# Gate and up products of the first 512 tokens between the attention steps of the last two token groups

## The chip, the cores and the metric

The kernel runs on one core of a Trainium2 chip. The metric is the device time of one execution in microseconds; before the change it is 2694.07 us, the median of three runs (2692.1 to 2694.11). PE is TensorE (PEld its weight loads), DVE is VectorE, ACT is ScalarE, POOL is GpSimd, and SP issues all the DMAs.

## What is computed

One layer of a hybrid encoder on 2048 tokens of width 1024, in float32: a normed input goes through one projection to a gated linear recurrence and to a stick-breaking attention with 8 heads of 64; both results are normed, projected and added to the input; then comes a gated feed-forward part with 2816 hidden channels and a last norm. Cut to what matters here:

```
h  = rms_norm(x) ;  u = h @ W_in                          # 1024 -> 2560
y  = concat(rms_norm(gelu(gate) * rg_lru(...)), rms_norm(stick_breaking_attention(q, k, v)))
x2 = x + y @ W_out
h2 = rms_norm(x2) ;  gu = h2 @ W_ffn_in                   # 1024 -> 2 * 2816
x3 = x2 + (silu(gu[:, :2816]) * gu[:, 2816:]) @ W_ffn_out
out = rms_norm(x3)
```

## The kernel before

Every float32 operand of a product is split into a high and a low part, and `mm3` (L115 to L118) takes three products for one: high by high, high by low, low by high.

The tokens are worked on in 4 groups of 512 (`GT`), g = 0 to 3. `prep(g)` takes the projections and the recurrence of a group. `attention(g)` takes its attention: an item is 128 queries of a head against up to 512 keys, and there are 32, 64, 96 and 128 items in the groups 0 to 3. For an item `score` (L317) makes the tile z on PE, ACT makes u and be of it by two sigmoids, `scan` (L336) runs the product of u along the keys on DVE, `weights` (L342) multiplies be by it on DVE, `turn` (L347) transposes be in 128x128 blocks on PE into t, which ACT (ah) and DVE (al) split, and `weigh` (L365) multiplies by the values on PE into y. `LAGS` says how many items score and scan run ahead of turn.

`drive` (L429) writes the steps of attention(g) and spreads units of other work, the fill, evenly between them. A unit is what the fill's generator does up to a `yield`. On PE the order stands as it is written; on the other engines a scheduler sets it. The fill of attention(0) to attention(2) is prep(1) to prep(3). The fill of attention(3) is `mix_out` (L668): for every group and branch but the last one it takes x + norm(y) @ W_out in `Mix.run` (L624), 32 units of 6 matmuls with 256 columns (tile po), and after a group's second branch `store_rows` (L655) writes the rows to DRAM (`x2_d`) and takes their norms (`rsf`). `next_half` (L225) hands out half a group of weight columns and starts the load of the half that is used two later (`AHEAD`); a half is 128x1024, loaded (raw), copied by ACT (hi) and subtracted by POOL in four pieces (lo), or loaded in its parts where an earlier use has kept them in DRAM.

After the attention the last branch is mixed, and the feed-forward part runs over two halves of 1024 tokens (`half`, each two groups of 512). `make_h2` (L752) loads, scales, transposes (h2t) and splits the rows of a half. For each of the 22 column tiles f, `gate_up` (L817) takes gate (j = 0) and up (j = 1): a 128x1024 tile of weights (gur, split into guh and gul by `split_gu`, L779) by both groups of the half, 24 matmuls with 512 columns into pgu for each group. Then silu, the product and its split into ahi and alo follow. `down` (L848) takes the second product (pw) for two column tiles at a time, one such pair behind `gate_up`. The weight tiles have three buffers (`wgu`), the raw tile has one.

```
        for g in range(NG - 1):
            drive(attention(g), prep(g + 1), n_prep - (g + 2 == NG) * LESS)
        n_out = 2 * TPG * (D // WC)
        drive(attention(NG - 1), mix_out(*first), n_out * (2 * NG - 1) + WAIT)
```

## Time and profile before

| | us |
|---|---|
| median of the timed runs | 2694.07 |
| span of the profiled execution | 7685.8 |
| PE busy in the profile | 7656.3 (100%) |
| DVE, ACT, POOL busy in the profile | 1421.4, 1124.6, 896.9 |

The profiled execution is 2.85 times as long as the timed ones. Its stretches, by the first scan of each group, are: start and prep(0) to about 460 us, attention(0) to 943, attention(1) to 1655, attention(2) to 2499, attention(3) to 3679, the last branch to 3789, the feed-forward part to the end. The durations that the profile gives for DVE, ACT and POOL are those of single instructions; how the ones of PE are to be read is a question of its own, since PE fills the whole span.

### The profile page before, as it was taken

How to read it: one execution, taken by the hardware profiler on the slowest of the kernel's cores; microseconds unless marked ns; L12 is line 12 of the kernel's file. 1: busy time of each engine (PE TensorE's matmuls, PEld its weight loads, DVE VectorE, ACT ScalarE, POOL GpSimd, SP SyncE). 2: the span in 40 equal slices, each digit the busy share in tenths (PEclk: the TensorE clock that was granted, in tenths of full speed). 3: DMA queues.
4: the chain of work that ended last, by engine and by line, in shares of the span. 5: the costliest groups of instructions: out<-in, count | busy, mean ns of one | idle time of the engine just before them, and what ended most of it. 6: DMA issues, size and time to landing. Idle time of an engine off the chain costs nothing.

```text
span 7685.8 us, 36652 instructions
## 1 busy us (share of the span) xinstructions
PE 7656.3 (100%) x13472; PEld 5024.0 (65%) x13472; DVE 1421.4 (18%) x2278; ACT 1124.6 (15%) x2024; POOL 896.9 (12%) x1261
## 2 busy tenths in 40 slices
PE   9999999999999999999999999999999999999999
PEld 5665676767676888888755555555555555555555
DVE  1112222223333333333100000000011000000002
ACT  2112212222222222222100000000011000000001
POOL 2211101100001110000010111111111111111111
DMA  3222222121111222211200000000011000000000
GB/s 106 78 82 73 92 71 69 59 71 55 56 59 61 68 76 66 76 50 49 79 19 14 19 19 18 18 19 19 17 36 55 19 19 17 19 19 19 17 17 25
DMA packets 167445, 350.05 MB, mean 46 GB/s; under 512 B 17504, under 2 KB 58464, under 8 KB 167264
## 3 DMA queue, kind: packets, MB, share of 16 engines
q1 hardware_dynamic: 167264, 347.70, 13.7%
q8 instruction: 106, 1.74, 0.1%
q14 instruction: 75, 0.61, 0.0%
HBM read 268.20 MB, written 79.43 MB: 45 GB/s over the span
## 4 chain that ended last, share of the span: by engine, by line
PE 100%; DVE 0%; DMA 0%; SPq 0%; issue 0%; ACT 0%
PE pgu L116 11%; PE pgu L117 11%; PE pgu L118 11%; PE y L375 6%; PE z L325 6%; PE t L360 6%; PE pw L117 6%; PE pw L116 5%; PE pj L116 5%; PE pj L118 5%; PE pw L118 5%; PE pj L117 5%; PE po L116 3%; PE po L117 3%; PE po L118 3%; PE pv L117 1%
## 5 line engine op out<-in xcount | busy, mean ns | idle before, releaser
L116 PE MATMUL pgu<-hhi,guh 128*128 128x512 f32 x1408 | 1201.0, 853 | 0.0
L117 PE MATMUL pgu<-hlo,guh 128*128 128x512 f32 x1408 | 1200.2, 852 | 0.0
L118 PE MATMUL pgu<-hhi,gul 128*128 128x512 f32 x1408 | 1200.1, 852 | 0.0
L116 PEld LDWEIGHTS pgu<-hhi,guh 128*128 128x128 f32 x1408 | 505.8, 359 | 363.1 <-issue 361.6
L117 PEld LDWEIGHTS pgu<-hlo,guh 128*128 128x128 f32 x1408 | 505.2, 359 | 360.6 <-issue 360.6
L118 PEld LDWEIGHTS pgu<-hhi,gul 128*128 128x128 f32 x1408 | 503.7, 358 | 362.9 <-issue 358.7
L116 PE MATMUL pj<-ht_hi,w_hi 128*128 128x512 f32 x512 | 601.0, 1174 | 0.0
L117 PE MATMUL pw<-dnl,ahi 128*128 128x512 f32 x704 | 587.9, 835 | 0.0
L118 PE MATMUL pw<-dnh,alo 128*128 128x512 f32 x704 | 587.6, 835 | 0.0
L116 PE MATMUL pw<-dnh,ahi 128*128 128x512 f32 x704 | 586.5, 833 | 0.0
L118 PE MATMUL pj<-ht_hi,w_lo 128*128 128x512 f32 x512 | 559.7, 1093 | 0.0
L117 PE MATMUL pj<-ht_lo,w_hi 128*128 128x512 f32 x512 | 559.0, 1092 | 0.0
L325 PE MATMUL z<-ks,qd 128*128 128x512 f32 (+2 forms) x640 | 552.6, 998 | 0.0
L360 PE MATMUL t<-ident,be 128*128 128x128 f32 x1088 | 534.3, 690 | 0.0
L830 DVE TENSOR_TENSOR sg<-pgu,sg 128x512 f32<-128x512 f32 x88 | 60.9, 692 | 2530.6 <-PE pgu L118 2516.7
L860 DVE TENSOR_TENSOR x<-pw,x 128x512 f32<-128x512 f32 x352 | 243.4, 692 | 987.0 <-PE pw L118 987.0
L360 PEld LDWEIGHTS t<-ident,be 128*128 128x128 f32 x1088 | 270.8, 249 | 234.2 <-issue 160.4
L785 POOL TENSOR_TENSOR gul<-gur,guh 128x1024 fp32r<-128x1024 f32 x88 | 208.0, 2364 | 1729.8 <-ACT guh L784 1635.4
L375 PE MATMUL y<-al,vs 128*128 128x256 f32 x576 | 395.7, 687 | 0.0
L375 PE MATMUL y<-ah,vs 128*128 128x256 f32 x576 | 395.0, 686 | 0.0
L116 PE MATMUL po<-wo_hi,yhi 128*128 128x256 f32 x512 | 384.2, 750 | 0.0
L118 PEld LDWEIGHTS pw<-dnh,alo 128*128 128x128 f32 x704 | 249.6, 355 | 172.8 <-issue 172.4
(183 smaller groups left out, 7820.4 us busy)
## 6 DMA issues: line engine op xcount, KB each, us to landing
gur<-in_w_gu SPq DMA_DIRECT2D x88, 512.0 KB, 3.4
w_hi<-w_d SPq DMA_DIRECT2D x50, 512.0 KB, 3.3
w_lo<-w_d SPq DMA_DIRECT2D x50, 512.0 KB, 4.6
dnr<-in_w_dn SPq DMA_DIRECT2D x88, 256.0 KB, 2.6
vs<-vs_d SPq DMA_DIRECT2D x80, 256.0 KB, 3.0
ks<-ks_d SPq DMA_DIRECT2D x80, 256.0 KB, 3.0
qd<-q_d SPq DMA_DIRECT2D x128, 128.0 KB, 2.8
w_raw<-in_w_in SPq DMA_DIRECT2D x30, 512.0 KB, 4.3
```

Source lines behind the costliest of these rows:

```text
L116: nc.tensor.matmul(ps, lhsT=w_hi, rhs=m_hi, start=first, stop=False)
L117: nc.tensor.matmul(ps, lhsT=w_hi, rhs=m_lo, start=False, stop=False)
L118: nc.tensor.matmul(ps, lhsT=w_lo, rhs=m_hi, start=False, stop=last)
L325: nc.tensor.matmul(z[:, :nz], lhsT=qd[:, i, qs], rhs=kss[p.c][:, :nz], start=i == 0, stop=i == 1)
L360: nc.tensor.transpose(tp[:, b, :], p.be[s][:, b * P:(b + 1) * P], ident)
L375: nc.tensor.matmul(y, lhsT=vs[:, b, :], rhs=t[:, b].rearrange("p s q -> p (s q)"), start=first and m == 0, stop=last and m == 1)
L785: nc.gpsimd.tensor_tensor(out=wlo, in0=raw, in1=f32(whi), op=ALU.subtract)
L830: nc.vector.tensor_tensor(out=sg, in0=pss[1, g], in1=sg, op=ALU.mult)
L860: nc.vector.tensor_tensor(out=x2[t][:, ns], in0=ps, in1=x2[t][:, ns], op=ALU.add)
```

## The change

The gate and up products of group 0, 22 x 2 x 24 matmuls with 512 columns, leave the feed-forward part. `gate_up_first` is a new piece of the fill: after the second branch of group 0 it scales the rows that are still on chip, transposes and splits them through `make_ht` (with the other gain and the tiles of the mixer), and takes the products of all 22 column tiles with weights from `next_half`; the gate is x * sigmoid(x) with ACT's sigmoid and one more product on DVE. The results go to `act_d` in DRAM, 256 KB each. The feed-forward part leaves group 0 out of `make_h2` and of the products and loads the results from `act_d`. The weights of the first half of the tokens are therefore loaded and split once more than before.

`mix_out` with `gate_up_first` now starts in attention(2): `OVER` = 96 units of it follow prep(3) there (4 empty ones, 64 of the branches of group 0, 8 of transposes and 20 of gate and up), and the rest, 332 units of gate and up and 160 of the other branches, is spread over attention(3), which had 228 units before. A unit of gate and up is 3 matmuls with 512 columns.

```diff
+OVER = 96
+    act_d = [dram.tile([P, GT], F32, name=f"act_d{f}") for f in range(NF)]
...
-    def make_ht(g, xs):
+    def make_ht(g, xs, gain=None):
+        gain = gm if gain is None else gain
...
-        nc.sync.dma_start(out=raw, in_=src)
+        dst = raw if src.shape[1] == KD // 2 else \
+            raw.rearrange("p k c -> p (k c)").rearrange("p (k c) -> p k c", c=src.shape[2])
+        nc.sync.dma_start(out=dst, in_=src)
...
+        if g == 0:
+            queue += [(w_gu[f, j], f"wgu{f}_{j}", ("gu", f, j), False) for f in range(NF) for j in range(2)]
...
-    def drive(steps, fill, n_fill):
+    def drive(steps, fill, n_fill, rest=True):
...
-        for _ in fill:
+        for _ in fill if rest else ():
             pass
...
+                    if self.rs is None:
+                        self.sums()
                     nc.vector.scalar_tensor_tensor(out=x2[t][:, ns], in0=po, scalar=self.rs[:, t:t + 1],
...
+    def gate_up_first(x2, last):
+        for t in range(TPG):
+            r = rsf[:, t:t + 1]
+            if t % 2:
+                nc.scalar.activation(x2[t], x2[t], AF.Copy, scale=r)
+            else:
+                nc.vector.tensor_scalar(out=x2[t], in0=x2[t], scalar1=r, scalar2=None, op0=ALU.mult)
+        yield from make_ht(NG, x2, gf)
+        for f in range(NF):
+            pss = []
+            for j in range(2):
+                hi, lo = (t.rearrange("p k c -> p (k c)").rearrange("p (k c) -> p k c", c=P) for t in next_half())
+                ps = ps_d.tile([P, GT], F32, tag="d", name=f"pgf{f}_{j}")
+                pss.append(ps)
+                for k in range(KD):
+                    mm3(ps, hi[:, k], lo[:, k], *hts[NG][k], k == 0, k == KD - 1)
+                    if k < KD - 1:
+                        yield
+                    elif (f, j) == (NF - 1, 1):
+                        last()
+                if j == 0:
+                    sg = stg.tile([P, GT], F32, tag="s", name=f"sgf{f}")
+                    nc.scalar.activation(sg, ps, AF.Sigmoid)
+                    nc.vector.tensor_tensor(out=sg, in0=ps, in1=sg, op=ALU.mult)
+                else:
+                    nc.vector.tensor_tensor(out=sg, in0=ps, in1=sg, op=ALU.mult)
+                    nc.sync.dma_start(out=act_d[f], in_=sg)
+                yield
...
-            yield from cur.run(x2, following, NCT if i + 2 < len(jobs) else NCT - 1)
+            gated = (g, br) == (0, 1)
+            yield from cur.run(x2, None if gated else following, NCT if i + 2 < len(jobs) else NCT - 1)
             if br == 1:
                 store_rows(g, x2)
+            if gated:
+                yield from gate_up_first(x2, lambda: [following.take(c) for c in range(NCT)])
...
-        for g in range(NG - 1):
-            drive(attention(g), prep(g + 1), n_prep - (g + 2 == NG) * LESS)
+        for g in range(NG - 2):
+            drive(attention(g), prep(g + 1), n_prep)
+        def filling():
+            yield from prep(NG - 1)
+            yield from mix_out(*first)
+        fill = filling()
+        drive(attention(NG - 2), fill, n_prep - LESS + OVER, rest=False)
...
-        drive(attention(NG - 1), mix_out(*first), n_out * (2 * NG - 1) + WAIT)
+        drive(attention(NG - 1), fill, n_out * (2 * NG - 1) + WAIT + KD + 2 * NF * KD - OVER)
...
+                if g == 0:
+                    hs.append(None)
+                    continue
...
-                for g, (hi, lo) in enumerate(hs):
+                for g, h in enumerate(hs):
+                    if h is None:
+                        continue
...
-                nc.scalar.activation(sg, pss[0, g], AF.Silu)
-                nc.vector.tensor_tensor(out=sg, in0=pss[1, g], in1=sg, op=ALU.mult)
+                if hs[g] is None:
+                    nc.sync.dma_start(out=sg, in_=act_d[f])
+                else:
+                    nc.scalar.activation(sg, pss[0, g], AF.Silu)
+                    nc.vector.tensor_tensor(out=sg, in0=pss[1, g], in1=sg, op=ALU.mult)
```

PE in the middle of attention(3), head 2, from one item's transposes to the next one's. Before, with branch 1 of group 0 as the fill:

```order
L360 MATMUL t3_2_0_2_0_11317<-ident_60,be3_2_0_2_0_11170 128x128 x4
L116 MATMUL po0_1_1_2_11290<-wo0_1_3_hi_10748,yhi0_1_0_1_10161 128x256
L117 MATMUL po0_1_1_2_11290<-wo0_1_3_lo_10749,yhi0_1_0_1_10161 128x256
L118 MATMUL po0_1_1_2_11290<-wo0_1_3_hi_10748,ylo0_1_0_1_10162 128x256
L116 MATMUL po0_1_1_2_11290<-wo0_1_3_hi_10748,yhi0_1_1_1_10168 128x256
L117 MATMUL po0_1_1_2_11290<-wo0_1_3_lo_10749,yhi0_1_1_1_10168 128x256
L118 MATMUL po0_1_1_2_11290<-wo0_1_3_hi_10748,ylo0_1_1_1_10169 128x256
L325 MATMUL z3_2_0_0_0_11333<-ks3_2_0_10559,qd3_2_10542 128x512 x2
L360 MATMUL t3_2_0_2_1_11340<-ident_60,be3_2_0_2_1_11201 128x128 x4
```

The same place on PE after the change, with the up product of column tile 9 (pgf9_1) as the fill:

```order
L368 MATMUL t3_2_0_2_0_12172<-ident_60,be3_2_0_2_0_12017 128x128 x4
L119 MATMUL pgf9_1_12188<-ht_hi4_0_10327,wgu9_1_hi_11987 128x512
L120 MATMUL pgf9_1_12188<-ht_lo4_0_10328,wgu9_1_hi_11987 128x512
L121 MATMUL pgf9_1_12188<-ht_hi4_0_10327,wgu9_1_lo_11988 128x512
L119 MATMUL pgf9_1_12188<-ht_hi4_1_10348,wgu9_1_hi_11987 128x512
L120 MATMUL pgf9_1_12188<-ht_lo4_1_10349,wgu9_1_hi_11987 128x512
L121 MATMUL pgf9_1_12188<-ht_hi4_1_10348,wgu9_1_lo_11988 128x512
L119 MATMUL pgf9_1_12188<-ht_hi4_2_10365,wgu9_1_hi_11987 128x512
L120 MATMUL pgf9_1_12188<-ht_lo4_2_10366,wgu9_1_hi_11987 128x512
L121 MATMUL pgf9_1_12188<-ht_hi4_2_10365,wgu9_1_lo_11988 128x512
L333 MATMUL z3_2_0_0_0_12201<-ks3_2_0_11417,qd3_2_11400 128x512 x2
L368 MATMUL t3_2_0_2_1_12208<-ident_60,be3_2_0_2_1_12043 128x128 x4
```

Between the two transposes stood 6 fill matmuls with 256 columns, and now there are 9 with 512.

PE at the place in attention(2) where the fill goes over from the second branch of group 0 (po0_1) to the transposes of its scaled rows (htp4, xo0), after the change:

```order
L119 MATMUL po0_1_1_3_10217<-wo0_1_3_hi_9764,yhi0_1_3_1_9308 128x256
L120 MATMUL po0_1_1_3_10217<-wo0_1_3_lo_9765,yhi0_1_3_1_9308 128x256
L121 MATMUL po0_1_1_3_10217<-wo0_1_3_hi_9764,ylo0_1_3_1_9309 128x256
L178 MATMUL htp4_0_10329<-ident_60,xo0_0_9135 128x128
L178 MATMUL htp4_0_10329<-ident_60,xo0_1_9137 128x128
L178 MATMUL htp4_0_10329<-ident_60,xo0_2_9139 128x128
L178 MATMUL htp4_0_10329<-ident_60,xo0_3_9141 128x128
L333 MATMUL z2_7_1_2_0_10337<-ks2_7_2_9552,qd2_7_9547 128x384 x2
```

The transposes stand directly behind the product whose result they turn, with no attention step between the two.

## Rows read from the trace of the kernel before

**Rows 1.** The page's head and PE's own busy time in it
```profile
span 7685.8 us, 36652 instructions
...
PE 7656.3 (100%) x13472; PEld 5024.0 (65%) x13472; DVE 1421.4 (18%) x2278; ACT 1124.6 (15%) x2024; POOL 896.9 (12%) x1261
```
**Rows 2.** Timeline in attention(3): start us, length us, engine, line, tiles, count
```profile
3001.27 3.10 PE L618 MATMUL pss<-ones,acc 128*128 128x1 f32 x8
```
**Rows 3.** Costliest PE groups: forms, count | busy us, mean ns | idle before
```profile
L116 PE MATMUL pgu<-hhi,guh 128*128 128x512 f32 x1408 | 1201.0, 853 | 0.0
...
L116 PE MATMUL pj<-ht_hi,w_hi 128*128 128x512 f32 x512 | 601.0, 1174 | 0.0
L117 PE MATMUL pw<-dnl,ahi 128*128 128x512 f32 x704 | 587.9, 835 | 0.0
...
L360 PE MATMUL t<-ident,be 128*128 128x128 f32 x1088 | 534.3, 690 | 0.0
...
L325 PE MATMUL z<-ks,qd 128*128 128x512 f32 x448 | 433.0, 1101 | 0.0
L375 PE MATMUL y<-al,vs 128*128 128x256 f32 x576 | 395.7, 687 | 0.0
...
L116 PE MATMUL po<-wo_hi,yhi 128*128 128x256 f32 x512 | 384.2, 750 | 0.0
```
**Rows 4.** Busy time by stretch: attention(2), attention(3), feed-forward part
```profile
core 0: us, PE busy (x) PEld busy (x) DVE busy (x) ACT busy (x) POOL busy (x), PEclk, DMA share, GB/s
...
1655.00:2499.00 844.00, 844.00 (x1503) 573.43 (x1502) 272.15 (x370) 203.59 (x382) 82.78 (x224) 1.00 0.18 58
2499.00:3679.00 1180.00, 1180.00 (x2644) 1017.33 (x2643) 402.11 (x634) 262.85 (x517) 95.26 (x263) 1.00 0.19 65
...
3789.00:7686.00 3897.00, 3886.89 (x6400) 2274.84 (x6399) 351.79 (x604) 294.71 (x453) 462.86 (x292) 1.00 0.07 23
```
**Rows 5.** PE groups by form in attention(3), 2499 to 3679 us
```profile
L116 PE MATMUL po<-wo_hi,yhi 128*128 128x256 f32 x448 | 337.9, 754 | 0.0
...
L360 PE MATMUL t<-ident,be 128*128 128x128 f32 x474 | 229.3, 685 | 0.0
L325 PE MATMUL z<-ks,qd 128*128 128x512 f32 x208 | 199.9, 1097 | 0.0
L375 PE MATMUL y<-ah,vs 128*128 128x256 f32 x252 | 173.0, 687 | 0.0
```
**Rows 6.** PE groups by form in attention(2), 1655 to 2499 us
```profile
L360 PE MATMUL t<-ident,be 128*128 128x128 f32 x337 | 165.6, 694 | 0.0
L116 PE MATMUL pj<-ht_hi,w_hi 128*128 128x512 f32 x126 | 155.5, 1234 | 0.0
...
L375 PE MATMUL y<-ah,vs 128*128 128x256 f32 x176 | 120.8, 686 | 0.0
```
**Rows 7.** Groups on POOL, ACT and DVE that the change adds or repeats
```profile
L785 POOL TENSOR_TENSOR gul<-gur,guh 128x1024 fp32r<-128x1024 f32 x88 | 208.0, 2364 | 1729.8 <-ACT guh L784 1635.4 <-DMA x_d<-xo 94.4
...
L196 POOL TENSOR_TENSOR w_lo<-w_raw,w_hi 128x256 fp32r<-128x256 f32 x120 | 90.5, 784 | 245.6 <-ACT w_hi L193 245.6
...
L830 DVE TENSOR_TENSOR sg<-pgu,sg 128x512 f32<-128x512 f32 x88 | 60.9, 692 | 2530.6 <-PE pgu L118 2516.7 <-ACT guh L784 13.9
...
L193 ACT CAST w_hi<-w_raw 128x1024 fp32r<-128x1024 f32 x30 | 31.1, 1045 | 84.8 <-PE pj L117 66.9 <-PE pv L118 9.2 <-issue 8.4
```
**Rows 8.** Timeline at the start of the feed-forward part, DVE and SP
```profile
3788.86 0.75 DVE L638 SCALAR_TENSOR_TENSOR xo<-po,ry_y,xo 128x512 f32<-128x512 f32 x1 [9.02 <-PE po L118]
...
3793.04 0.17 DVE L665 COPY rsf<-rf_y 128x4 f32<-128x4 f32 x1
...
3794.63 4.20 SPq L872 DMA_DIRECT2D x<-x_d  x8
...
3799.86 0.33 SPq L781 DMA_DIRECT2D gur<-in_w_gu  x1
```

**Rows 9.** DMA issues on the page: count, KB each, median us to landing
```profile
gur<-in_w_gu SPq DMA_DIRECT2D x88, 512.0 KB, 3.4
```

More of the change, by code (lines that the diff above doesn't have):

```diff
@@ L174, in make_ht @@
                 nc.tensor.transpose(tp[:, t * P:(t + 1) * P], xs[t][:, k * P:(k + 1) * P], ident)
-            nc.scalar.activation(hi, tp, AF.Copy, scale=gm[:, k:k + 1])
-            nc.vector.scalar_tensor_tensor(out=lo, in0=tp, scalar=gm[:, k:k + 1], in1=f32(hi),
+            nc.scalar.activation(hi, tp, AF.Copy, scale=gain[:, k:k + 1])
+            nc.vector.scalar_tensor_tensor(out=lo, in0=tp, scalar=gain[:, k:k + 1], in1=f32(hi),
                                            op0=ALU.mult, op1=ALU.subtract)
@@ L622, in sums @@
             self.rs = rsqrt_mean(ss, TPG, LRU, f"ry{self.nm}")
+        rs = None
         def run(self, x2, following=None, ready=NCT):
@@ L757, in make_h2 @@
             yield hs
-            for gl, (hi, lo) in enumerate(hs):
+            for gl, h in enumerate(hs):
+                if h is None:
+                    continue
+                hi, lo = h
                 g = half * (HT // GT) + gl
@@ L820, in gate_up @@
                 whi, wlo = early.pop((half, f, j), None) or load_gu(half, f, j)
-                for g, (hi, lo) in enumerate(hs):
+                for g, h in enumerate(hs):
+                    if h is None:
+                        continue
+                    hi, lo = h
                     ps = pss[j, g] = ps_g.tile([P, GT], F32, tag="p", name=f"pgu{half}_{f}_{j}_{g}")
```

## The prediction

> **What bounds the kernel now.** I read the page's head first, and it does not fit the times: the span is 7685.8 us, PE is busy in all of it [rows 1], and the timed runs take 2694.07 us. So the next question is what a PE duration in this profile means. A timeline in attention(3) tells: eight matmuls with a single column take 3.10 us, 0.39 us each [rows 2]. 13472 matmuls [rows 1] at 0.39 us would be 5254 us, twice the timed runs. The profiled execution thus has a cost per PE instruction that the timed ones cannot have. PE's busy share, and every wait for PE, is a product of the profiling here and tells nothing of the timed runs. The reader who takes "PE 100%" at its word would say that moving PE work gains nothing; that is a rival below.
>
> What holds in both are instruction counts, shapes, and the lengths on DVE, ACT and POOL. So I price PE by columns. The large groups have 2.16 (pgu, three lines of 1408), 1.08 (pw), 0.79 (pj), 0.14 (t), 0.23 (z), 0.29 (y, two lines of 576) and 0.39 million columns (po) [rows 3]; pv and other small groups add 0.34 by the code's loops: 5.42 million. **Upper price:** PE cannot work for longer than the run, so a column costs on average at most 2694.07 us / 5.42 million = 0.497 ns. **Lower price:** the stretches show a granted clock of 1.00 [rows 4], the 2.4 GHz level; one column in one of its cycles would be 0.417 ns. No row shows that it is one cycle, so I keep both ends. At the lower price PE works 2259 us and is idle for 435 us; at the upper one never.
>
> Where could it be idle? attention(3): po has 1344 matmuls of 256, t 474 of 128, z 208 of 512 (and some shorter), y 504 of 256 [rows 5], in all 0.66 million columns, 276 to 330 us. DVE is busy there for 402.11 us [rows 4]. attention(2): pj 378 of 512, t 337, y 352 [rows 6], with z, pv and small ones by the code 0.48 million columns, 199 to 238 us, against 272.15 us on DVE [rows 4]. In the feed-forward part it is the other way: 3.24 million columns, 1352 to 1612 us, against 351.79 us on DVE [rows 4]. So in the last two groups of attention DVE needs longer than PE at either price, and in the feed-forward part PE is alone. The floors of the two groups are DVE's 402 + 272 = 674 us, of which PE stands for 106 (upper price) to 199 us (lower).
>
> **The change part by part.** *Removed:* 1056 matmuls of 512 columns and 32 transposes leave the part where PE is the bound: 0.545 million columns, 227 (lower) to 271 us (upper).
>
> *Added to attention(2):* 64 units of po, 8 of transposes and 20 of gate and up, 0.13 million columns or 55 to 66 us. PE comes to 254 to 304 us, DVE to about 290 (272 plus the po sums and splits that move over). New floor 290 to 304.
>
> *Added to attention(3):* 332 units of gate and up come (0.51 million columns), 64 units of po go (0.10). PE comes to 448 to 534 us. DVE pays the 44 products of the gate and up at 0.692 us [rows 7], 30 us in all, and loses the po sums that left: about 420 us. PE is the bound now, at 448 to 534.
>
> The two floors together go from 674 to 738 (lower price) or 838 us (upper), a growth of 64 to 164 us, against 227 to 271 removed: **163 us gained at the lower price, 107 at the upper.**
>
> *Covers.* Each of the 44 halves of weights is loaded (512 KB, 3.4 us to landing [rows 9]), copied by ACT (1.045 us) and subtracted by POOL in 4 pieces of 0.784 us [rows 7]: 7.6 us one after the other. It is started two halves ahead, that is 48 matmuls of 512 columns, at least 10 us, and the attention steps between them. Covered; bare, it would be 44 x 7.6 = 334 us. ACT's 46 us and POOL's 138 us fit: in attention(3) ACT is busy for 262.85 and POOL for 95.26 us [rows 4], in some 470 us to come. On POOL a piece of 0.784 us may stand ahead of a mask of the attention; score runs four items ahead, so I put it at nothing. The 22 stores to and loads from act_d are 256 KB each on SP's queue, 11 MB beside the 77 MB (65 GB/s over 1180 us, [rows 4]) that attention(3) moves anyway: nothing. In the first half of the feed-forward part each weight tile now covers 24 matmuls and not 48; the split's longest piece, 2.364 us on POOL [rows 7], stands four times in a pair of column tiles that takes PE at least 41 us: covered.
>
> *New waits, once each.* (1) The hand-over in attention(2): the transposes of group 0's rows stand on PE directly behind the last po. From the last sum xo to the end of the norm chain (rsf) it is 4.3 us at the end of the mixer [rows 8]; the scaling and the first split come after it. 6 to 10 us, and since PE keeps its order, the attention steps queued behind wait too. (2) The way back: the next branch's inputs can be split only when the last gate and up products let go of the tiles: 2 to 4 us. (3) At the start of the feed-forward part eight loads of 512 KB (x) stand on SP ahead of the fourth weight tile, whose load is issued 11.0 us after the last sum [rows 8]; landing and split bring it to some 20 us. It was needed after 6 x 24 matmuls (31 us), and now after 3 x 24 (15 us): about 5 us. Together 15 to 25 us; I take 20.
>
> **Sum.** The profiled execution's own span cannot carry it, being 2.85 times too long, so the sum is made against the median of 2694 us: 163 - 20 = 143 gained at the lower price, 107 - 20 = 87 at the upper. The middle is 115; I take **2580 us**. Neither end alone is likely: the upper leaves no idle PE anywhere in 2694 us, which DVE's floors contradict; the lower takes narrow matmuls and transposes at their columns, which no row shows.
>
> What the narrow instructions cost is the weak point: in the profile a transpose of 128 columns takes 690 ns and a matmul of 256 takes 687 [rows 3], the profile's own cost again. The Trainium skill (TensorE: Matmul & The Clock Gate, Part 4) has about 275 ns for a 128x128 transpose in a kernel's context. No run here shows it. By it the 474 and 337 transposes would bring PE to 381 and 274 us before the change, nearly DVE's floors, and the time after it would come out at about 2690 us.
>
> **The rivals.** *More than the floors* (the two groups wait more than DVE's sum, and the denser fill covers it). Of the 435 us of idle PE at the lower price, 199 are in these floors; 236 lie elsewhere. By DVE's share (674 of 1421 us, [rows 1, 4]) 111 of them would be waits from item to item in these two groups, over z, sigmoid, scan, product and transpose. If half of that vanishes under 9 matmuls of fill where 6 short ones stood, the time is 2694 - 143 - 55 = 2496 us. For it: each item is a chain through four engines. Against it: score already runs four items ahead. The Trainium skill (the same page, Part 1) says that PE's clock falls to half in idle stretches and comes back with activity; the rows show 1.00 everywhere, but of a PE that the profile keeps busy. By that rule a denser fill would add to this rival's gain.
>
> *PE is full already: slower.* If the 435 us are no idle time but a surcharge on the 4800 or so matmuls with 256 columns or fewer, each costs 0.09 us more. attention(3) has 2322 of them (po, y, t), so PE takes 276 + 210 = 486 us there, more than DVE, and what is moved comes back in full: 2694 + 20 = 2714 us. It decides from (402 - 276) us / 2322 = 0.054 us of surcharge on. For it: "PE 100%" on the page and narrow instructions as dear as wide ones. Against it: nothing would then be left for the start and the end.
>
> *Weights late.* SP takes its queue in order, and keys and values of the next head wait there for buffers. If each of the 33 halves used in attention(3) comes 2.5 us late, 80 us of the 115 go: 2660 us.
>
> *No difference.* The floors' gain is eaten by waits, as with the dear transposes above: 2690 us.
>
> **Chances.** Forecast 0.62 (2550 to 2610), more than the floors 0.14 (about 2496), weights late 0.08 (2660), no difference 0.05 (2690), PE full 0.11 (2714). The range of 2485 to 2675 takes in the first three and leaves out the last two and the ends of the others. A measurement can tell about 0.2% (5 us) from no change; faster 0.84, the same 0.05, slower 0.11.
>
> **What would show it.** The span of the profile after should stay near 7700 us or grow, since it has as many matmuls and its PE cost goes by instructions: the profile itself will not show the gain. Right: no long wait of PE for the gate and up weights, DVE near 420 us in attention(3), one idle stretch of PE at htp4 of 6 to 10 us. Wrong: waits of PE for POOL's w_lo of the gate and up (weights late), or a time over 2694 us with the floors as computed (PE full). Taking the gate and up products out of the fill altogether would show on the clock what they cost there.

## The result, and the profile after

The changed kernel takes 2657.71 us (median of four runs, 2654.95 to 2660.74) against 2693.09 us for the kernel before (four runs). The ratio is 0.9868, with a 95% interval of 0.9854 to 0.9882: 35 us, or 1.3%, faster. The forecast was 2580 us, 114 us faster. The sign was right and the time lies in the range, but the gain is less than a third of the forecast.

The profile of the changed kernel is not stretched: its span is 2659.0 us, as long as the timed runs. The one that the prediction rested on was (7685.8 us, [rows 1]). So with the experiments the kernel before was profiled once more (before_again), and that profile is of the true length too. All readings from here on compare these two. The heads of the two pages, before_again first:

```profile
span 2691.3 us, 36652 instructions
...
PE 2557.8 (95%) x13472; PEld 2169.7 (81%) x13472; DVE 1404.6 (52%) x2278; ACT 1084.1 (40%) x2024; POOL 907.8 (34%) x1261
```
```profile
span 2659.0 us, 37282 instructions
...
PE 2553.9 (96%) x13472; PEld 2175.3 (82%) x13472; DVE 1453.5 (55%) x2298; ACT 1128.2 (42%) x2066; POOL 1059.9 (40%) x1437
```

The number of PE instructions is the same, and so is their busy time. PE was busy for 95% of the run before the change; by these records 133.5 us of PE were idle in the whole kernel. After the change 105.1 us are left. The forecast wanted 114 us.

Where it went is told by the busy time by stretch of attention(2), attention(3) and the feed-forward part (columns as in [rows 4]), of before_again and then of the changed kernel:

```profile
core 0: us, PE busy (x) PEld busy (x) DVE busy (x) ACT busy (x) POOL busy (x), PEclk, DMA share, GB/s
513.00:790.00 277.00, 250.54 (x1508) 212.74 (x1507) 262.28 (x369) 195.93 (x386) 84.35 (x224) 0.99 0.56 179
790.00:1184.00 394.00, 350.49 (x2627) 324.02 (x2628) 383.18 (x636) 247.59 (x511) 94.56 (x262) 0.99 0.58 192
1221.00:2691.00 1470.00, 1447.47 (x6402) 1195.03 (x6400) 361.15 (x604) 292.49 (x453) 467.32 (x292) 1.00 0.18 61
```
```profile
513.00:854.00 341.00, 313.18 (x1980) 277.65 (x1979) 301.75 (x445) 223.12 (x431) 125.19 (x269) 0.96 0.60 198
854.00:1381.00 527.00, 522.94 (x3240) 464.84 (x3239) 412.49 (x612) 287.62 (x542) 207.04 (x393) 0.99 0.48 163
1412.00:2659.00 1247.00, 1213.34 (x5348) 999.35 (x5346) 345.57 (x582) 277.07 (x432) 466.87 (x292) 0.99 0.22 76
```

| | before | after | change |
|---|---|---|---|
| attention(2) and (3), length | 671 | 868 | +197 |
| of it PE busy | 601.0 | 836.1 | +235 |
| of it PE idle | 70.0 | 31.9 | -38 |
| feed-forward part, length | 1470 | 1247 | -223 |
| of it PE busy | 1447.5 | 1213.3 | -234 |
| of it PE idle | 22.5 | 33.7 | +11 |
| between them (1184 to 1221, 1381 to 1412) | 37 | 31 | -6 |

-223 + 197 - 6 = -32 us, which is the difference of the spans. In a sentence: 235 us of PE's busy time moved, and only 38 us of it fell into idle PE, since the two groups had only 70; in the feed-forward part 11 us of new idle time came up. Busy time is more than PE's work, since a record is longer than the step to the next matmul. Counted by those steps (the prices in the part on the prediction below), PE's work in the two groups was 568 of 671 us before and is 810 of 868 us now: 103 us were free, where the forecast's two prices gave 106 and 199, and 45 of them were filled.

In attention(3) PE is now full (522.94 of 527 us). In attention(2) it is not: 28 us of it idle, as before (26.5). The longest waits of PE there (engine, line and tile that waited, what for: us in total, times, longest) are these:

```profile
PE htp L178 <- DVE xo L686: 11.1, 1, 11.1
PE t L368 <- DVE al L370: 6.2, 7, 3.3
PE t L368 <- DVE ry_y L108: 3.9, 1, 3.9
PE z L333 <- ACT be L338: 3.3, 2, 2.0
```

The first is the hand-over that the prediction named: the transposes of group 0's rows stand behind the last sum and the norm. PE's waits at the start of the feed-forward part (1405 to 1440 us) are those for the weight tiles (ACT's copy guh and POOL's remainder gul):

```profile
PE pgu L119 <- ACT guh L843: 5.6, 1, 5.6
PE pgu L121 <- POOL gul L844: 1.2, 1, 1.2
```

### The profile page after: what moved, and what is told of

The parts are those of the page before. It is cut to its first block, busy times and chain, and to the rows that moved or that the text cites. A ratio compares the mean times of both kernels' runs of the same rounds, so it can differ in the third digit from the quotient of the medians.

```text
span 2659.0 us, 37282 instructions
## 1 busy us (share of the span) xinstructions
PE 2553.9 (96%) x13472; PEld 2175.3 (82%) x13472; DVE 1453.5 (55%) x2298; ACT 1128.2 (42%) x2066; POOL 1059.9 (40%) x1437
## 4 chain that ended last, share of the span: by engine, by line
PE 75%; DVE 9%; ACT 3%; POOL 3%; issue 2%; DMA 2%; SPq 0%; POOLq 0%; DVEq 0%; ACTq 0%
PE pgu L121 9%; PE pgu L120 9%; PE pgu L119 9%; PE pw L121 6%; PE pw L120 6%; PE pw L119 6%; PE y L383 4%; PE z L333 3%; PE t L368 3%; PE pgf L119 3%; PE pgf L121 3%; PE pgf L120 3%; DVE u L347 2%; PE po L119 2%; PE po L121 2%
## 5 line engine op out<-in xcount | busy, mean ns | idle before, releaser
L119 PE MATMUL pgu<-hhi,guh 128*128 128x512 f32 x1056 | 411.9, 390 | 5.6 <-ACT guh L843 5.6
L121 PE MATMUL pgu<-hhi,gul 128*128 128x512 f32 x1056 | 412.2, 390 | 5.1 <-POOL gul L844 5.1
L120 PE MATMUL pgu<-hlo,guh 128*128 128x512 f32 x1056 | 411.8, 390 | 0.0
L119 PE MATMUL pw<-dnh,ahi 128*128 128x512 f32 x704 | 275.3, 391 | 1.0 <-DVE x L925 1.0
L121 PE MATMUL pw<-dnh,alo 128*128 128x512 f32 x704 | 275.3, 391 | 0.0
L120 PE MATMUL pw<-dnl,ahi 128*128 128x512 f32 x704 | 274.8, 390 | 0.3 <-POOL dnl L910 0.3
L119 PEld LDWEIGHTS pgu<-hhi,guh 128*128 128x128 f32 x1056 | 198.8, 188 | 47.3 <-ACT guh L843 6.0
L119 PE MATMUL pj<-ht_hi,w_hi 128*128 128x512 f32 x512 | 213.2, 416 | 2.1 <-DVE sl L266 1.5
L121 PE MATMUL pj<-ht_hi,w_lo 128*128 128x512 f32 x512 | 201.7, 394 | 0.0
L120 PE MATMUL pj<-ht_lo,w_hi 128*128 128x512 f32 x512 | 201.4, 393 | 0.0
```

The costliest lines, as they stand in the source:

```text
L119: nc.tensor.matmul(ps, lhsT=w_hi, rhs=m_hi, start=first, stop=False)
L120: nc.tensor.matmul(ps, lhsT=w_hi, rhs=m_lo, start=False, stop=False)
L121: nc.tensor.matmul(ps, lhsT=w_lo, rhs=m_hi, start=False, stop=last)
```

## Experiments

**First set: was there little idle PE, or did new waits eat it?** Two theories stood against each other. The first: there was little idle PE before. The second: the idle PE was there as forecast, and new waits took the gain.

*before_again*, the kernel before, unchanged.

> The kernel before once more, for a profile whose span is near its timed 2693 us. In the profile after, PE starts matmuls of 512, 256 and 128 columns 227, 119 and 109 ns apart, and the feed-forward part takes 1247 us. Theory 1 (little idle PE before): the feed-forward part takes 1247 + 1056 x 0.227 = about 1487 us, so attention(2) and attention(3) take about 660 us together (868 after), with PE needing some 560 of them: idle PE of only 95 to 105 us, most of it in attention(3). Theory 2 (the idle was there as forecast, 150 us or more, and new waits after the change ate it): the two groups take 700 us or more before.

Measured: 2693.05 us, with the span and the stretches above. PE is busy for 601 us of the two groups, where the forecast had 475 to 568, and DVE for 645 us, where the stretched profile had 674 [rows 4]. The two groups take 671 us, where the first theory said about 660 and the second 700 or more, and 103 us of them are free of PE's work, where the first said 95 to 105. That speaks for the first theory.

*b_po2 and a_po2*: the third product of each mixer step is left out (low part of the input by high part of the weights), in the kernel before and in the changed one: 512 matmuls of 256 columns less.

```diff
-                            mm3(po[:, i * WC:(i + 1) * WC], yh[:, ts], yl[:, ts], hi[:, c], lo[:, c],
-                                c == 0, c == NCT - 1)
+                            pc = po[:, i * WC:(i + 1) * WC]
+                            nc.tensor.matmul(pc, lhsT=yh[:, ts], rhs=hi[:, c], start=c == 0, stop=False)
+                            nc.tensor.matmul(pc, lhsT=yh[:, ts], rhs=lo[:, c], start=False, stop=c == NCT - 1)
```

> The kernel before without the third product (low rows by high weights) in the mixing of the branches: 512 matmuls of 256 columns less, at 0.119 us 61 us of PE work, 53 of it in attention(3) and 8 behind it; the output is not the reference's. If DVE sets the pace of attention(3) before the change (the forecast's floors), the time falls by the 8 us and little more: 2693 to 2675-2685. If PE sets it, it falls by 50 to 60: 2633 to 2643.

> The changed kernel without the same third product, 61 us of PE work less: 15 in attention(2), 38 in attention(3), 8 behind it. PE is the bound in attention(3) after the change, so both theories say 38 + 8 us at the least, 2612 or less; attention(2) gives its 15 us if PE is the bound there too (2597), and nothing if DVE is.

Measured: b_po2 2676.56 us, ratio 0.9935 (0.9920 to 0.9949), 18 us less than the kernel before (2694.61 beside it); a_po2 2630.32 us, ratio 0.9765 (0.9750 to 0.9780), 27 us less than the changed one. The 512 matmuls are worth 61 us of PE at 0.119 us each. Before the change three tenths of that show on the clock: DVE holds attention(3) there. The row of attention(3) in b_po2:

```profile
790.00:1172.00 382.00, 306.69 (x2168) 280.65 (x2167) 375.76 (x632) 250.12 (x510) 106.67 (x261) 0.95 0.59 197
```

382 us with DVE busy for 375.76: 53 us of PE were taken out of the group, and it is 12 us shorter. So DVE did set the pace of attention(3), as forecast; but PE stood close behind it (350 of 394 us). After the change more of the same 61 us shows, but not all: attention(3) fell by 18 us only, from 527 to 509, and attention(2) by 7. Both theories had at least 46 us for this run, and both were wrong. Attention(3) has two parts after the change: first the fill is gate and up, then, from the last of these products on, it is the mixing of the other branches. The two parts in the changed kernel:

```profile
854.00:1200.00 346.00, 346.00 (x1838) 291.87 (x1837) 256.16 (x322) 187.96 (x340) 169.81 (x312) 1.00 0.40 132
1200.00:1381.00 181.00, 176.94 (x1403) 172.97 (x1403) 156.33 (x291) 99.67 (x203) 37.23 (x81) 0.98 0.64 221
```

In a_po2 the first part is 344 us long. In the second, where all the left-out products of the group were, DVE now sets the pace:

```profile
1191.00:1356.00 165.00, 144.56 (x1100) 137.54 (x1098) 153.33 (x295) 99.64 (x207) 39.71 (x81) 0.97 0.70 245
```

165 us instead of 181, for 38 us of PE.

*a_few*: the changed kernel with only one of the eight steps of each gate and up product in the fill (924 matmuls of 512 columns less; the output is without them).

```diff
-                    mm3(ps, hi[:, k], lo[:, k], *hts[NG][k], k == 0, k == KD - 1)
+                    if k == KD - 1:
+                        mm3(ps, hi[:, k], lo[:, k], *hts[NG][k], True, True)
```

> The changed kernel with only the last of the 8 steps over k of each gate and up product in the fill: 308 x 3 = 924 matmuls of 512 columns less, 210 us at 0.227; everything else (weights, their splits, sigmoid, products, stores, the order) stays, and the output is not the reference's. Theory 1: the two groups fall back to DVE's pace, some 690 us, so the time falls by about 170 us, to 2490. Theory 2: the waits that came with the weights and the products stay, the time falls by less than 130 us, to 2530 or more.

Measured: 2583.73 us, ratio 0.9593 (0.9577 to 0.9609), 74 us less than with the products, for 210 us of PE (924 x 0.227). By its time alone the run is on the side of the second theory. The rows of the two parts of attention(3), and PE's longest wait in the group, tell more:

```profile
856.00:1118.00 262.00, 178.57 (x950) 147.81 (x950) 252.84 (x313) 181.78 (x335) 200.55 (x306) 0.87 0.52 169
1118.00:1306.00 188.00, 178.57 (x1403) 173.92 (x1402) 162.46 (x300) 103.61 (x210) 38.61 (x86) 0.96 0.65 220
...
PE t L368 <- DVE be L353: 62.5, 34, 3.6
```

Attention(3) takes 450 us without the products, where the kernel before took 394. In the first part, with hardly any gate and up on PE, DVE is busy for 253 of 262 us and sets the pace. The steps of the attention are spread evenly over the units of fill, 332 of gate and up and 160 of mixing, so by estimate two thirds of 394 us, 266, would be the pace of the kernel before: there the group did fall back to DVE's pace, as the first theory said. The second part does not: it is 188 us long against an estimate of 128, with PE busy for 179. The mixing used to be spread over the whole group; the 160 units of it that are left for attention(3) stand in its last third, and PE sets the pace there, with or without the gate and up products. What the products cost on the clock are the 84 us by which the first part shortened (346 to 262). Attention(2) is 342 us long, as with the products (341), but only 39 of the 1056 had stood in it. So the run speaks for the first theory in attention(3); why attention(2) is 341 us long is the question of the second set.

**Second set: what holds attention(2)?** My theory at this point was that attention(2) has no idle PE that this fill can use (A); its rival, that it does take fill in, and that its growth is the hand-over and other new waits (B). OVER says how many units of the new fill stand there.

> The kernel after with OVER = 0: none of the new fill stands in attention(2) any more, all of it in attention(3). The 96 units that move are 64 of po (6 matmuls of 256 columns at 119 ns, 46 us), 8 of transposes (3.5 us) and 20 of gate and up (3 of 512 at 227 ns, 13.6 us): 63 us of PE. Theory A (attention(2) has no idle PE that such fill can use; a unit there costs what it takes on PE, and attention(3) is full on PE): attention(2) goes back to 275 to 282 us, attention(3) rises by 55 to 65 us, and the time stays within 10 us of 2658. Theory B (attention(2) did take in a part of its 41 us of idle PE, and what it grew by is the hand-over and other new waits, which move along): the time rises by 15 to 40 us, to 2673 to 2698.

> The kernel after with OVER = 192: 96 more units of gate and up (3 matmuls of 512 columns at 227 ns, 0.68 us, 65 us together) stand in attention(2) and leave attention(3). Theory A: attention(2) rises by about 65 us to some 405 us with its 44 us of idle PE still there; attention(3) falls to about 465 us (513 - 65 = 448 of PE need against 412 of DVE), and the time stays within 10 us of 2658. Theory B (a denser fill would take in the idle PE of attention(2)): attention(2) rises by 25 to 45 us only and the time falls by 20 to 40 us, to 2618 to 2638.

```diff
-OVER = 96
+OVER = 0
```

Measured: with OVER = 0, 2679.17 us, ratio 0.9945 (0.9932 to 0.9957), 21 us more than with 96; with OVER = 192 (the same line), 2640.14 us, ratio 0.9805 (0.9792 to 0.9818), 18 us less. Theory A falls, on both sides; the gain with 192 is just short of theory B's 20 to 40 us. The rows of attention(2) and (3), OVER = 0 first:

```profile
513.00:791.00 278.00, 253.31 (x1519) 215.71 (x1519) 263.20 (x372) 196.90 (x388) 85.28 (x225) 0.98 0.56 180
791.00:1401.00 610.00, 588.34 (x3704) 526.93 (x3703) 448.88 (x686) 315.74 (x587) 248.59 (x437) 0.98 0.51 170
```
```profile
511.00:898.00 387.00, 369.19 (x2248) 323.93 (x2247) 319.05 (x457) 235.58 (x445) 166.08 (x314) 0.98 0.60 194
898.00:1362.00 464.00, 459.55 (x2969) 412.40 (x2968) 398.79 (x601) 272.62 (x527) 173.35 (x347) 1.00 0.52 169
```

Idle PE in the two groups together: 46 us with OVER = 0, 32 with 96, 22 with 192. With 192 the load of PE in attention(2) is 50 us above DVE's, and 18 us of PE are idle; with 96 the loads are 313 and 302, and 28 are idle; with 0 DVE's is the larger, and 25 are idle.

*a_pause*: 12 empty units of fill ahead of the transposes, so that attention steps stand on PE while the norm is worked out.

```diff
+        for _ in range(12):
+            yield
         yield from make_ht(NG, x2, gf)
```

> The kernel after with 12 empty units of fill between the scaling of group 0's rows and their transposes (OVER counts 12 more, so that the split between the two groups stays): attention steps stand on PE while the norm of the rows is worked out. If the one wait of PE for the scaled rows (11.1 us in the profile after) is all that the hand-over costs: 8 to 11 us less, 2647 to 2650, and the wait of the transposes under 2 us. If attention(2) is held by DVE around it anyway (the attention steps put in its place wait in turn): under 3 us less, 2655 to 2659, with the idle time of PE at z and t in its stead.

Measured: 2654.55 us, ratio 0.9856 (0.9843 to 0.9870), 3 us less, which is within the spread of the runs. PE waits at the same place nearly as long as before:

```profile
PE t L370 <- DVE al L372: 10.2, 10, 2.8
PE htp L180 <- DVE xo L688: 10.0, 1, 10.0
```

The norm's small instructions ran in one piece on DVE in the changed kernel, from 1.1 us after the last sum on (821.7 to 827.2 us). Here the scans and products of the attention stand ahead of them and between them: they begin 9.8 us after the last sum (817.2 us, the sum ends at 807.4). What was filled on PE was lost to the norm.

*a_x2late*: the eight loads of x for the first half of the feed-forward part are written behind its first two column tiles.

```diff
+            if half:
+                load_x2()
...
                 acts = [gate_up(half, f, hs) for f in fs]
+                if not x2:
+                    load_x2()
```

> The kernel after with the eight loads of x (512 KB each) of the first half of the feed-forward part written behind the gate and up of its first two column tiles, so that the third and fourth weight tile are loaded ahead of them. If the waits at the start of that part (pgu for guh 5.6 us, for gul some 5 us, and the gaps at pgu of 7.8 us in all) come from these loads: 4 to 10 us less, 2648 to 2654. If the one buffer of the raw weight tile (load, ACT's copy, POOL's split one after the other) sets them: within 3 us of 2658.

Measured: 2650.68 us, ratio 0.9839 (0.9825 to 0.9852), 7 us less: these loads were the cause of that much. The timeline of SP in the changed kernel shows them (start us, length us, line, what is issued, count), and the longest pieces of the critical chain how long the weight tile behind them took to land:

```profile
1418.36 5.21 SPq L937 DMA_DIRECT2D x<-x_d  x8
1424.60 0.33 SPq L840 DMA_DIRECT2D gur<-in_w_gu  x1
```
```profile
1418.36 6.17 DMA x<-x_d
1424.60 11.36 DMA gur<-in_w_gu
```

The prediction gave that load 3.4 us [rows 9]; behind 4 MB of x it takes 11.36. In a_x2late PE has no wait for a weight tile in the first 30 us of the feed-forward part, and the part is 1240 us long instead of 1247. In the 30 us behind, PE still waits for guh (1.5 us) and gul (2.4). What the start cost in all is told by its first 60 us, of before_again and then of the changed kernel:

```profile
1221.00:1281.00 60.00, 60.00 (x267) 49.69 (x266) 5.86 (x20) 16.14 (x23) 24.41 (x14) 1.00 0.48 172
```
```profile
1412.00:1472.00 60.00, 49.28 (x205) 38.55 (x204) 5.16 (x19) 16.83 (x25) 28.02 (x17) 0.94 0.55 200
```

62 matmuls fewer in the same time are 14 us at 0.227 us each; a_x2late has 235 of them there, so it gives half of it back.

**Third set: DVE's load, and what the better places add up to.**

*a_relief*: in attention(2) POOL takes every second product of be by u from DVE.

```diff
-        nc.vector.tensor_tensor(out=p.be[s][:, :n], in0=p.be[s][:, :n], in1=p.u[s][:, 1:n + 1], op=ALU.mult)
+        eng = nc.gpsimd if p.g == NG - 2 and s else nc.vector
+        eng.tensor_tensor(out=p.be[s][:, :n], in0=p.be[s][:, :n], in1=p.u[s][:, 1:n + 1], op=ALU.mult)
```

> The kernel after (OVER = 96), but in attention(2) the product be by u of every second query tile (48 items of 96, 0.68 us each on DVE) is taken by POOL instead, which is busy for 125 of the 341 us there; POOL's products of 512 columns take 1.66 us, 80 us together. DVE has then some 268 us of work in attention(2) instead of 301, PE 297 as before. Theory C (attention(2) is longer than either engine's work because PE and DVE have nearly the same load, 297 and 301, and each waits for the other in turn): with DVE relieved, attention(2) falls from 341 by 15 to 25 us, the time to 2633 to 2643. Theory D (the chain from item to item, not DVE's load, sets it; POOL's product is 1 us longer and stands in a queue with masks and splits): no gain or a loss, 2655 to 2680.

Measured: 2658.90 us, ratio 0.9868 (0.9855 to 0.9882), no difference. Two groups of DVE in attention(2), of the changed kernel and of this one (count | busy us, mean ns | idle before), show why this is no clean test of DVE's load:

```profile
L347 DVE TENSOR_TENSOR_SCAN u<-u,u,zero 128x513 f32<-128x513 f32 x64 | 85.5, 1337 | 8.0 <-ACT u L337 8.0
...
L475 DVE SCALAR_TENSOR_TENSOR xc<-xpad,lp,xc 128x512 f32<-128x512 f32 x12 | 8.9, 743 | 0.1
```
```profile
L347 DVE TENSOR_TENSOR_SCAN u<-u,u,zero 128x513 f32<-128x513 f32 x64 | 89.3, 1397 | 12.9 <-ACT u L337 12.8
...
L476 DVE SCALAR_TENSOR_TENSOR xc<-xpad,lp,xc 128x512 f32<-128x512 f32 x12 | 10.6, 882 | 0.1
```

48 products left DVE, but its busy time fell by 17 us only (302 to 284): the 48 products had taken some 34, and others of its instructions became longer while POOL worked beside it. And the first scan of a chain now waits 24.7 us for POOL's masks instead of 16.6, since these share POOL's queue with the products. Relief that goes through POOL is eaten by both. Whether DVE's load alone would do it stays open.

*best192, best256, best192p*: OVER = 192 and the later loads of x; the same with 256; the same with 192 and 32 empty units at the hand-over.

> OVER = 192 and the loads of x written later, together. The two act in different stages (attention(2) and (3), start of the feed-forward part), so the gains of 17.6 and 7.0 us should add: 2633 (2630 to 2637). If the later loads only move the wait to somewhere that OVER = 192 changes too: 2638 to 2642.

> OVER = 256 and the loads of x written later. PE need moves by another 44 us: attention(2) some 402 us of PE against 330 of DVE, attention(3) 408 of PE against 391 of DVE. Theory C (a group is held at the greater load only where one engine is clearly ahead): attention(3) now has two nearly equal loads and gets idle PE, as attention(2) had at OVER = 96; its length is 425 to 440 and the time 2633 to 2650, no better than with 192. Theory E (it is the place only: fill in attention(2) finds idle PE, at any density): another 10 to 15 us less than with 192, 2617 to 2624.

> As with OVER = 192 and the later loads, with 32 empty units of fill ahead of the transposes of group 0's rows (12 gave 3.1 us, and 10 us of the wait were left, since the norm's instructions then stood behind those of attention on DVE). If only the pause was too short: the wait for the scaled rows goes from 9 us to under 2, and the time falls by 4 to 9 us against the same kernel without it, to 2624 to 2629. If the attention steps in the pause run at DVE's pace and leave PE idle as long: within 3 us of it, 2630 to 2636.

Measured: best192 2633.67 us, ratio 0.9775 (0.9762 to 0.9789); the two gains add to the microsecond, and no version is faster, 60 us under the kernel before. best256 2647.04, ratio 0.9828 (0.9814 to 0.9841): 13 us worse. Its attention(2) and (3):

```profile
512.00:945.00 433.00, 413.21 (x2431) 360.98 (x2430) 327.80 (x464) 245.14 (x456) 185.39 (x345) 0.98 0.57 185
945.00:1374.00 429.00, 419.35 (x2785) 380.44 (x2784) 387.11 (x593) 262.92 (x515) 141.13 (x317) 0.99 0.52 171
```

Now it is attention(3) that has idle PE again (10 us instead of 4), while attention(2) still has 20. That fits theory C in the text above, that a group comes near its PE work only where this stands well above DVE's, and theory E falls. It does not show theory C by itself: attention(2) has 20 us of idle PE here although PE leads by a quarter, 11.7 us of them the wait at the hand-over. best192p 2642.57, ratio 0.9806 (0.9793 to 0.9820), is 9 us worse than best192 and outside of both expectations: the wait for the scaled rows is still 6.5 us (8.9 without the pause), and PE's waits for al there grow from 4.7 to 8.7 us.

**Fourth set: the hand-over by itself.**

*a_nohand* leaves out the scaling of group 0's rows by their norm, so that the transposes need only the sums. *a_later* keeps the rows in tiles that the recurrent branch has let go of, and puts the transposes behind the first branch of group 1, nothing left out. *best192h* and *best224h* are best192 with this, and with OVER = 192 and 224.

```diff
-            gated = (g, br) == (0, 1)
+            gated = (g, br) == (1, 0)
...
                 store_rows(g, x2)
+                if g == 0:
+                    scale_first(x2)
+                    rows0 = x2
...
-                yield from gate_up_first(x2, lambda: [following.take(c) for c in range(NCT)])
+                yield from gate_up_first(rows0, lambda: [following.take(c) for c in range(NCT)])
```

> The kernel after without the scaling of group 0's rows by their norm: the rows are transposed as they are, so PE no longer waits for the norm (the computation leaves out this scaling). In the profile after PE waits 11.1 us for the scaled rows, and the granted clock is 0.56 and 0.75 in the two stretches of 10 us at and behind it. If the hand-over is a cost of its own in attention(2): 9 to 14 us less than 2658, 2644 to 2649. If attention(2) is held by other things at this place and the wait only stands in for them: under 4 us less, 2654 to 2659.

> The kernel after with the hand-over moved: group 0's rows stay in tiles that the recurrent branch has let go of, are scaled when their norm is done, and are transposed only behind the first branch of group 1 (32 units of po later), so the norm has some 40 us. OVER = 96 as before. Nothing is left out. If the hand-over is a cost of its own: 8 to 14 us less than 2658, 2644 to 2650, without the wait for xo. If the wait reappears elsewhere (attention(2) held by DVE at this place): within 4 us of 2658.

> OVER = 192, the later loads of x and the moved hand-over together (without the last it was 2633.7). If the hand-over's 9 us of wait and its slower clock go: 2620 to 2627. If not: 2630 to 2636.

> As the one before with OVER = 224. Some 22 us of PE more move from attention(3) (then about 430 of PE against 393 of DVE) to attention(2). If a group keeps PE full while PE's load is some 10% above DVE's: the same as with 192 or up to 6 us less, 2616 to 2627. If attention(3) already gets idle PE there, as with OVER = 256: 2 to 8 us more than with 192.

Measured: a_nohand 2655.56 us, ratio 0.9855 (0.9841 to 0.9868), 2 us less, within the spread of the runs. PE still waits at the transposes. The timelines of PE, DVE and ACT show why:

```profile
829.62 1.08 PE L178 MATMUL htp<-ident,xo 128*128 128x128 f32 x4 [8.39 <-DVE rf_b L106]
```
```profile
821.48 0.66 DVE L95 TENSOR_SCALAR rf_v<-ssg 128x4 f32<-128x4 f32 x1
...
828.74 0.74 DVE L180 SCALAR_TENSOR_TENSOR ht_lo<-htp,gf,ht_hi 128x512 fp32r<-128x512 f32 x1
```
```profile
823.18 1.88 ACT L179 ACTIVATE ht_hi<-htp,gf 128x512 fp32r<-128x512 f32 x3
```

The transposes write to a pool of three tiles (ps_d). Three tiles of them are done and copied by ACT by 825.1 us; the fourth needs a tile back, and DVE gives the first one back at 829.48, since its ht_lo stands behind the norm's instructions. So leaving out the scaling does not take the norm out of the way: the run does not test what the hand-over costs. a_later 2650.23, ratio 0.9835 (0.9821 to 0.9848), 7.5 us less, and the wait for the scaled rows is gone:

```profile
PE t L368 <- DVE al L370: 11.6, 10, 3.3
PE htp L178 <- DVE ht_lo L180: 4.1, 6, 1.3
```

So at OVER = 96 the hand-over is a cost of its own of 7 to 8 us, less than its wait of 11.1; PE's waits for al rise from 6.2 to 11.6 us in its place. In best192h, 2635.49 us (ratio 0.9778, 0.9765 to 0.9792), nothing of it is left against best192 (2633.67): attention(2) is 4 us shorter, attention(3) 3 us longer. best224h, 2639.78 (0.9792, 0.9778 to 0.9805), is 4 us worse than that, at the edge of the noise.

## Why the prediction was right in sign and wrong in size

**The stretched profile** was read rightly: PE's 100% in it told nothing, and the rival "PE is full already" fell, since the time went down. It had a part of the truth, though: PE was busy for 95% of the true run, and narrow instructions do cost more by the column than wide ones (below). It was also expected that the profile after would be as long (near 7700 us). It was 2659.0; the stretching belongs to that one profile, not to the kernel.

**The term that failed most is the growth of the floors, and two steps behind it failed: DVE's floor was taken from the stretched profile, and PE was priced by columns**, one price for every matmul, taken in the middle of 0.417 and 0.497 ns. Back-to-back rows of the changed kernel and of before_again give each form's own (start us first, then the length of a record):

```profile
1429.73 0.40 PE L121 MATMUL pw<-dnh,alo 128*128 128x512 f32 x1
1429.96 0.39 PE L119 MATMUL pw<-dnh,ahi 128*128 128x512 f32 x1
```
```profile
902.13 0.29 PE L117 MATMUL po<-wo_lo,yhi 128*128 128x256 f32 x1
902.25 0.28 PE L118 MATMUL po<-wo_hi,ylo 128*128 128x256 f32 x1
902.37 0.60 PE L360 MATMUL t<-ident,be 128*128 128x128 f32 x4
902.73 0.37 PE L116 MATMUL po<-wo_hi,yhi 128*128 128x256 f32 x1
902.94 0.28 PE L117 MATMUL po<-wo_lo,yhi 128*128 128x256 f32 x1
```

A matmul of 512 columns starts 0.23 us after the one before it (0.227 over longer rows: 0.443 ns a column), one of 256 after 0.12 (0.119: 0.465 ns). Four transposes take 0.36 us, and the matmul behind them 0.21 instead of 0.12: 0.45 us in all, 0.11 for each or some 0.85 ns a column. So the wide matmuls of the feed-forward part lie near the lower price and the two groups, with their narrow ones, at the upper. With these prices, summed over the forms of each stretch, PE's work in the two groups was 237 + 331 = 568 us before; the forecast's middle was 522, its upper price 568. The upper price was set aside because it "leaves no idle PE anywhere"; that is so only if it holds for the wide matmuls too. An argument about the mean over the run was used against a value for a part of it.

The sum, term by term:

- *Removed*: 227 to 271 us forecast, 249 in the middle; 1056 x 0.227 = 240 measured (the 32 transposes, some 4 us, are left out here and in the feed-forward part below). 9 us of the miss.
- *Growth of the floors*: 64 to 164 us forecast, 114 in the middle. Measured (PE's work first, then DVE's): before max(237, 263) + max(331, 383) = 646; after max(297, 302) + max(513, 412) = 815; growth 169. 55 us of the miss, the largest term. 28 of these are DVE's floor: its 674 us [rows 4] of the stretched profile are 645 in the true one, so the groups had less of a floor to grow from. 22 are PE's price in attention(3), 513 against 491 in the middle, and 5 are attention(2). With the 9 us above, the price by columns makes 31 of the miss.
- *That a group goes down to its floor*: before the change the two were 25 us longer than their floors, after it 53. The prediction had 8 to 14 us for that, the hand-over and the way back. 28 against that is 14 to 20 us of the miss. This term is what is left over between the lengths and the floors. The hand-over's wait of 11.1 us was forecast (6 to 10), and is worth 7.5 us by a_later. Most of the rest sits in attention(2), where PE's busy time (313) and DVE's (302) are nearly equal. That the near equality is the cause was not shown: a_relief was no clean test.
- *Start of the feed-forward part*: 5 us forecast, 240 - 223 = 17 measured for the whole part, 14 of them in its first 60 us. The cause was named rightly (eight loads of x ahead of a weight tile) for the 7 us that a_x2late gives back; the landing was mis-sized there, 11.36 us, not 3.4. The rest are further waits for weight tiles and a lower clock (0.94 over the first 60 us).
- *Not forecast*: the last branch between the groups and the feed-forward part is 6 us shorter.

240 - 169 - 28 - 17 + 6 = 32, the difference of the spans. One slip of adding softened the miss: the three new waits of the prediction, 6 to 10, 2 to 4 and 5 us, make 13 to 19 us and not "15 to 25".

**The covers** held. The loads and splits of the 44 halves of weights cost PE no wait that the trace shows: the rival "weights late" fell. DVE's 412 us in attention(3) were forecast as about 420, PE's 523 as 448 to 534.

**The rival "no difference"**, by transposes that are dear, had the right direction. The Trainium skill (TensorE: Matmul & The Clock Gate, Part 4) has about 275 ns for a transpose. The trace agrees if that is the length of one record: 272 ns in the middle of the 472 transposes of attention(3) in before_again. As a price it does not hold here, since their records overlap and they cost 0.11 us each. The forecast with that figure as a price, 2690 us, was too slow; the forecast with columns was too fast.

```profile
L360 PE MATMUL t<-ident,be x472: 270/272/477, 790.1 to 1180.7; 128*128 128x128 f32 x158
```

**The rival "more than the floors"** fell: the groups stayed above their floors, and further than before.

## What to carry to other kernels

Before work is moved into idle time, measure that idle time in a profile as long as the timed runs: a gain of 115 us was added up where 103 us were free, and 45 of them could be filled. Price each form of instruction from back-to-back rows of that form, since a mean over the run is too dear for wide matmuls and too cheap for narrow ones and transposes. Read a group of steps part by part where its fill changes: the engine that sets the pace may change with it. Do not count on a group coming down to the work of the longer engine: attention(3) came within 1 to 4% of it, but attention(2) was 9% above it with nearly equal busy times (313 and 302), and still 5% with leads of PE of 16% and 26%. So try several splits of the fill, and look at the first loads behind each seam.

## What the runs showed of the hardware

- The same kernel has profiles of 7685.8 and of 2691.3 us. In the long one a matmul of one column is 0.39 us, and PE is busy throughout. DVE's busy time in the two groups is 674 us there and 645 in the short one, though its instructions are no shorter (the lengths of 1003 of them add up to 705 and 714 us): in the short one they stand closer, and a record often begins some 0.08 us before the one ahead of it ends.
- The granted clock falls where PE stands still. The stretches around the hand-over of the changed kernel:

```profile
810.00:820.00 10.00, 6.86 (x55) 6.48 (x53) 8.81 (x14) 7.12 (x19) 0.96 (x6) 1.00 0.50 160
820.00:830.00 10.00, 1.40 (x5) 0.81 (x5) 7.67 (x19) 3.95 (x6) 5.34 (x9) 0.56 0.43 157
830.00:840.00 10.00, 9.59 (x54) 8.46 (x54) 8.73 (x12) 8.90 (x17) 2.73 (x4) 0.75 0.07 26
840.00:850.00 10.00, 10.00 (x58) 8.51 (x57) 9.66 (x12) 6.22 (x12) 0.77 (x7) 1.00 0.70 262
```

  With PE busy for 1.4 of 10 us the clock goes to 0.56 of the 2.4 GHz level, near the lower one of 1.2 GHz, and it is at 0.75 for the next 10 us with PE busy again. In a_few, with PE busy for 357 of 450 us, it was 0.91 over all of attention(3), against 0.99 in the changed kernel. The prediction had no row to price this with, since its profile showed 1.00 everywhere. No run tells the clock's share of the cost from the wait's: a_later took both away and gained 7.5 us.
- POOL's products make DVE's instructions longer: 743 to 882 ns for one of 512 elements, in a_relief. The Trainium skill (GPSIMD Engine Reference, 1. Specifications) says that the two share an interface to the SBUF and contend for it with instructions of two inputs there; this agrees: DVE's remainders al, which have one operand in PSUM, did not become longer (612 and 608 ns).
